# A part of one load is moved to GpSimd's queue: 1536 columns in 75, 9 and 44 partitions, after tile 53 is cast

## The chip, the cores and the metric

One core of a Trainium2 chip. The time is that of one execution on the device, in microseconds (us). The core has a TensorE (PE; its weight loads are PEld), a VectorE (DVE), a ScalarE (ACT), a GpSimd (POOL), a sync engine (SP) that issues most transfers, and 16 DMA engines that carry them. A program on fewer than eight cores has one state as a rule; all runs told of here are fast ones, and only these are compared.

## The reference

```python
def setup_inputs():
    batch, m, k, n = 16, 512, 1024, 768
    # x [16,512,1024], weight [1024,768], sub_value [16,512,768], all float32
def reference(x, weight, sub_value):
    return (np.matmul(x, weight) - sub_value).astype(np.float32)
```

Flattened, x has 8192 rows, 64 tiles of 128. The kernel reads 34 MB of x, 3 MB of weight and 25 MB of sub_value, and writes 25 MB.

## The kernel before

Eight tiles form a segment; a partition's 8 rows of a segment lie side by side in memory, so that one transfer of 8 tiles of x is 128 runs of 32 KB. The list of transfers is issued in this order by the sync engine ('x', 's', 'o' are loads of x, loads of sub_value and stores of the result; first tile, count). 'p' is the one exception: it goes to GpSimd's queue, in three parts.

```python
    ('x', 48, 8), ('s', 48, 8), ('x', 56, 7), ('p', 63, 1),
    ('o', 24, 8), ('o', 32, 8), ('s', 56, 8), ('o', 40, 8), ('o', 48, 8), ('o', 56, 5),
    ('o', 61, 2), ('o', 63, 1),
...
PARTS = (120, 125), (0, 120), (125, 128)
...
            if kind == "p":
                here, there = x_ring[:, at % NX], view(x_flat, at, 1)[:, 0]
                waits, landed["x", at] = [(counter["cast"], cast_at[at - NX]), *landed["x", at - 1]], []
                for low, high in PARTS:
                    sem = tc.alloc_semaphore(f"part{low}")
                    pool.add(lambda low=low, high=high, here=here, there=there: nc.gpsimd.dma_start(
                        out=here[low:high], in_=there[low:high], max_dma_last_dim=2048,
                    ), waits, (sem, 16))
                    landed["x", at].append((sem, 16))
                continue
```

So tile 63 of x (4 KB per partition) waits until tiles 56 to 62 have landed. ScalarE casts each tile to float16, TensorE or VectorE transposes it, TensorE multiplies, VectorE subtracts (the loads of sub_value and the stores share one ring of 32 tiles), and the sync engine stores.

## Time and profile before

| | before |
|---|---|
| median of 3 runs | 210.59 us (210.33 to 210.60) |
| span of the profiled run | 208.6 us |
| TensorE busy | 94% of the span |
| DMA | 87.08 MB at 417 GB/s |
| last matmul ends, last subtraction ends | 201.49, 202.47 us |
| last store: first and last of its 16 counts | 205.13, 207.32 us |

A transfer raises its semaphore sixteen times, once for each DMA engine that has done its share. When such counts lie far apart, some engine is behind. GpSimd's issue stands in the timeline of its engine (start, duration, what, the idle time before it and what ended it):

```profile
162.45 2.00 POOL L265 DMA_DIRECT2D x_ring<-in_x_dram  x3 [136.72 <-DMA x_ring<-in_x_dram]
```

and its landing in the list of issues (KB each, us from issue to landing):

```profile
x_ring<-in_x_dram SPq DMA_DIRECT2D x1, 3584.0 KB, 21.9
...
x_ring<-in_x_dram POOLq DMA_DIRECT2D x1, 480.0 KB, 14.7
...
x_ring<-in_x_dram POOLq DMA_DIRECT2D x1, 20.0 KB, 6.8
x_ring<-in_x_dram POOLq DMA_DIRECT2D x1, 12.0 KB, 15.8
```

One part of 120 partitions carries nearly all of it; the two small ones seem to be there to move the place at which the next part begins.

### The profile page before, as it was taken

Reading aid. Unit: us, or ns where it says so; the run is one execution under the profiler, and the core shown is the slowest. Engines: PE = TensorE matmul, PEld = TensorE weight load, DVE = VectorE, ACT = ScalarE, POOL = GpSimd, SP = SyncE. Lnnn points to the kernel's source line nnn. Section 1 sums busy time; section 2 is a strip of 40 time slices with the busy share of each in tenths; the row PEclk is TensorE's granted clock in tenths of the full one; section 3 lists DMA queues with packets and bytes.
Section 4 is the critical chain, followed back from the end, with each engine's and each line's share of the span. In section 5 each row is a group of like instructions: output and inputs, shape, how many; then the busy total and the mean of one; then the engine's idle time right before and its main releaser. Section 6 shows DMA issues by size and latency. Waiting matters only on the chain.

```text
span 208.6 us, 2617 instructions
## 1 busy us (share of the span) xinstructions
PE 195.2 (94%) x1234; PEld 75.4 (36%) x700; DVE 128.1 (61%) x224; ACT 109.0 (52%) x113; POOL 3.0 (1%) x10
## 2 busy tenths in 40 slices
PE   6899699969999999999999999999999999999960
PEld 0233244324434433443443443344344344344310
DVE  2233224975993895597399389469739938942330
ACT  2655659506573761854745676183574746516300
POOL 1000000000000000000000000000000300000000
PEclk9999999999999999999999999999999999999997
DMA  6999999999999999999999999999999999999993
GB/s 204 421 428 429 437 423 431 449 435 427 424 440 446 371 443 433 444 421 411 455 440 427 415 429 448 430 452 404 424 441 428 433 432 423 443 424 433 421 418 155
DMA packets 5685, 87.08 MB, mean 417 GB/s; under 512 B 689, under 2 KB 689, under 8 KB 2097
## 3 DMA queue, kind: packets, MB, share of 16 engines
q1 hardware_dynamic: 5472, 86.51, 97.3%
q0 software_dynamic: 208, 0.52, 0.6%
q14 instruction: 4, 0.02, 0.0%
q8 instruction: 1, 0.02, 0.0%
HBM read 61.87 MB, written 25.17 MB: 417 GB/s over the span
## 4 chain that ended last, share of the span: by engine, by line
PE 75%; DMA 13%; DVE 6%; SPq 3%; issue 1%; DVEq 0%
PE po_b L200 67%; DMA so_ring<-in_sub_value_dram 13%; PE pt_b L348 8%; DVE xtp_b L381 3%; DVE so_ring L430 2%; SPq L311 2%; SPq L275 1%; SPq L566 0%; DVEq L61 0%; SPq L140 0%
## 5 line engine op out<-in xcount | busy, mean ns | idle before, releaser
L200 PE MATMUL po_b<-w_sb,xt_b 128*128 128x384 f16 x704 | 126.0, 326 | 0.9 <-DVE w_sb L278 0.8
L430 DVE TENSOR_TENSOR so_ring<-po_b,so_ring 128x768 f32<-128x768 f32 x64 | 60.7, 957 | 58.9 <-PE po_b L200 39.8
L361 ACT COPY xt_b<-pt_b 128x1024 f16<-128x1024 f16 x44 | 44.5, 1012 | 64.7 <-PE pt_b L348 63.8
L381 DVE STREAM_TRANSPOSE xtp_b<-x16p_b 32x256 f32<-32x256 f32 x144 | 62.7, 435 | 2.3
L200 PE MATMUL po_b<-w_sb,xtp_b 128*128 128x384 f16 x320 | 61.3, 326 | 1.8 <-DVE xtp_b L381 1.7
L410 PEld LDWEIGHTS <-xt_b 128*128 128x128 f16 x352 | 34.4, 98 | 58.4 <-issue 55.2
L330 ACT CAST x_b<-x_ring 128x1024 f16<-128x1024 f32 x46 | 47.2, 1048 | 5.5 <-DMA x_ring<-in_x_dram 5.5
L348 PE MATMUL pt_b<-ident,x_b 128*128 128x128 f32 x184 | 47.6, 274 | 1.9 <-ACT x_b L330 1.9
L348 PEld LDWEIGHTS pt_b<-ident,x_b 128*128 128x128 f32 x184 | 25.3, 141 | 45.0 <-issue 36.3
L330 ACT CAST x16p_b<-x_ring 128x1024 f16<-128x1024 f32 x18 | 18.8, 1046 | 14.8 <-DMA x_ring<-in_x_dram 14.8
L410 PEld LDWEIGHTS <-xtp_b 128*128 128x128 f16 x160 | 15.7, 98 | 20.3 <-issue 18.3
L278 DVE CAST w_sb<-so_ring 128x768 f16<-128x768 f32 x8 | 4.1, 557 | 12.0 <-DMA so_ring<-in_weight_dram 12.0
L200 PE MATMUL po_b<-idle_x,idle_w 128*128 128x512 f16 x26 | 7.7, 443 | 1.7 <-POOL idle_x L180 1.7
L265 POOL DMA_DIRECT2D x_ring<-in_x_dram x3 | 2.0, 668 | 136.7 <-DMA x_ring<-in_x_dram 136.7
L361 ACT COPY xtp_b<-pt_b 128x1024 f16<-128x1024 f16 x2 | 2.0, 1012 | 2.4 <-PE pt_b L348 2.4
L330 ACT ACT_TABLE_LOAD x1 | 1.3, 1283 | 0.9 <-SPq L140 0.9
L440 PEld LDWEIGHTS <-idle_w 128*128 128x128 f16 x4 | 0.4, 100 | 1.7 <-POOL idle_x L180 1.7
L189 DVE TENSOR_TENSOR ident<-along,across 32x32 f32<-32x32 f32 x4 | 0.7, 183 | 0.1
L181 DVE MEMSET ones<- 128x32 f32 x1 | 0.1, 85 | 1.0 <-SPq L140 1.0
L180 POOL MEMSET idle_x<- 128x512 f16 x1 | 0.5, 531 | 0.0
L489 POOL MEMSET mark<- 128x1 f32 x1 | 0.1, 99 | 24.0 <-ACT xtp_b L361 24.0
L512 ACT CAST stub<-ident 128x1 f16<-128x1 f32 x2 | 0.4, 194 | 0.0
(8 smaller groups left out, 1.2 us busy)
## 6 DMA issues: line engine op xcount, KB each, us to landing
so_ring<-in_sub_value_dram SPq DMA_DIRECT2D x7, 3072.0 KB, 24.2
out_dram<-so_ring SPq DMA_DIRECT2D x7, 3072.0 KB, 26.6
x_ring<-in_x_dram SPq DMA_DIRECT2D x4, 4096.0 KB, 21.6
x_ring<-in_x_dram SPq DMA_DIRECT2D x2, 2048.0 KB, 27.2
x_ring<-in_x_dram SPq DMA_DIRECT2D x1, 3584.0 KB, 21.9
so_ring<-in_weight_dram SPq DMA_DIRECT2D x4, 768.0 KB, 8.8
x_ring<-in_x_dram SPq DMA_DIRECT2D x1, 3072.0 KB, 28.3
x_ring<-in_x_dram SPq DMA_DIRECT2D x2, 1024.0 KB, 24.8
```

Source lines behind the costliest of these rows:

```text
L189: dve.add(lambda here=here: nc.vector.tensor_tensor(out=ident[here, here], in0=along[here], in1=across[here], op=mybir.AluOpType.is_equal, ...
L200: return nc.tensor.add_instruction(mybir.InstMatmult(name=nc.get_next_instruction_name(), engine=full.engine, ins=list(full.ins), outs=lis ...
L265: pool.add(lambda low=low, high=high, here=here, there=there: nc.gpsimd.dma_start(out=here[low:high], in_=there[low:high], max_dma_last_di ...
L275: sp.add(lambda st=st, at=at: nc.sync.dma_start(out=st, in_=w_c[at]), then=(sem, 16))
L278: lambda at=at, r=r, st=st: nc.vector.tensor_copy(out=w_sb[:, at, r], in_=st[:, r]),
L311: sp.add(lambda here=here, there=there: nc.sync.dma_start(out=here, in_=there), waits, (sem, 16))
L330: act.add(lambda: nc.scalar.copy(out=to, in_=x_in), waits, count("cast"))
L348: pe.add(lambda: nc.tensor.transpose(words, from_, ident), waits, count("turn") if last else None)
L361: act.add(lambda: nc.scalar.copy(out=to, in_=pt_b[:, b]), waits, count("evac"))
L381: dve.add(lambda: nc.vector.transpose(xt[b * Q : (b + 1) * Q, :, a * Q : (a + 1) * Q], x16[a * Q : (a + 1) * Q, :, b * Q : (b + 1) * Q],), ...
L410: pe.add(lambda weights=weights: nc.tensor.ldweights(weights, tile_position=(0, 0)), [w for w in waits if w[0] in ready])
L430: dve.add(lambda: nc.vector.tensor_tensor(out=o, in0=po[:, :, :NS], in1=o, op=mybir.AluOpType.subtract), [*landed["s", mi], (counter["mul" ...
```

## The change

GpSimd takes 1536 columns instead of 1024 (1.5 tiles: half of tile 62 and tile 63), waits for a cast instead of for the landing of the load before, and deals the rows out in other parts. The intent can be read from the numbers: the parts give some DMA engines more rows than others.

```diff
-    ... ('x', 56, 7), ('p', 63, 1),
+    ... ('x', 56, 8),
-PARTS = (120, 125), (0, 120), (125, 128)
+PARTS_AT, PARTS_AFTER, PARTS_OF = 56, 53, 1536
+PARTS = (0, 75), (75, 84), (84, 128)
 ...
-            if kind == "p":            # (cut: the whole branch goes)
 ...
+            if (kind, at) == ("x", PARTS_AT):
+                here, there = here.rearrange("p j c -> p (j c)"), there.rearrange("p j c -> p (j c)")
+                whole = n * K - PARTS_OF
+                parts = [(tc.alloc_semaphore(f"part{low}"), 16) for low, _ in PARTS]
+                for t in range(at + whole // K, at + n):
+                    landed["x", t] = [*landed["x", t], *parts]
+
+                def own(here=here[:, whole:], there=there[:, whole:]):
+                    for (low, high), part in zip(PARTS, parts):
+                        pool.add(lambda low=low, high=high: nc.gpsimd.dma_start(
+                            out=here[low:high], in_=there[low:high], max_dma_last_dim=2 * PARTS_OF,
+                        ), [(counter["cast"], cast_at[PARTS_AFTER])], part)
+
+                later[PARTS_AFTER] = own
+                here, there = here[:, :whole], there[:, :whole]
 ...
+        later.pop(mi, lambda: None)()      # in cast(mi)
```

## The prediction

> **What bounds the kernel now.** I read the page from the top: busy shares, the 40 slices, the DMA queues, the chain that ended last; then the waits of the last 70 us, the windows of the tail, the landing times, and last the single DMA packets.
>
> The slices and the queue table say which resource is full:
>
> ```profile
> PE   6899699969999999999999999999999999999960
> DMA  6999999999999999999999999999999999999993
> GB/s 204 421 428 429 437 423 431 449 435 427 424 440 446 371 443 433 444 421 411 455 440 427 415 429 448 430 452 404 424 441 428 433 432 423 443 424 433 421 418 155
> q1 hardware_dynamic: 5472, 86.51, 97.3%
> q0 software_dynamic: 208, 0.52, 0.6%
> ```
>
> Two resources are full. TensorE works without a gap from about 45 us to 201.5 us, and the 16 DMA engines are at 9 tenths or more in every slice but the first and last, at some 430 GB/s. GpSimd's queue (q0) carries 0.52 MB of 87 MB.
>
> The windows and waits of the tail say which one sets the end:
>
> ```profile
> 190.00:200.00 10.00, 10.00 (x66) 3.89 (x37) 3.83 (x4) 3.98 (x4) 0.00 (x0) 1.00 1.00 428
> 200.00:208.60 8.60, 1.48 (x10) 0.29 (x3) 0.96 (x1) 0.00 (x0) 0.00 (x0) 0.84 0.61 257
> ...
> POOL x_ring L265 <- DMA x_ring<-in_x_dram: 136.7, 1, 136.7
> DVE so_ring L430 <- DMA so_ring<-in_sub_value_dram: 2.7, 1, 2.7
> SPq L537 <- DMA out_dram<-so_ring: 3.4, 1, 3.4
> ```
>
> The columns of the first two are PE, PEld, DVE, ACT, POOL, clock, DMA share, GB/s. After 200 us TensorE has 1.48 us left, while the DMA engines are still busy. The chain of work ends with the last subtraction, 201.51 to 202.47 us; yet the last store, issued at 202.50, lands 4.8 us later:
>
> ```profile
> 196.28 5.21 PE po_b L200 x32
> 201.51 0.96 DVE so_ring L430
> ...
> out_dram<-so_ring SPq DMA_DIRECT2D x1, 1920.0 KB, 10.4
> out_dram<-so_ring SPq DMA_DIRECT2D x1, 768.0 KB, 6.5
> out_dram<-so_ring SPq DMA_DIRECT2D x1, 384.0 KB, 4.8
> ```
>
> 384 KB at 430 GB/s is 0.9 us, so most of the 4.8 us is backlog. I joined the trace's DMA packets from 155 us on into 16 chains (a packet of one DMA engine starts within 4 ns of the end of the one before; only 4 of 1449 joints are irregular). No chain has a gap of note before the end: every engine works through the last three stores back to back, ending at 204.79, 204.84, 204.90, 205.00, 205.02, 205.08, 205.17, 205.21, 205.24, 205.45, 205.55, 205.73, 206.20, 206.70, 206.76 and 207.00 us. The last semaphore count is at 207.32 and the closing instructions take 1.3 us more. So **the end is set by the latest of 16 equally fast DMA engines**. Their mean end is 205.54: perfect balance would be worth 1.46 us, 0.7% of the time, and this is the only thing that the change can win, since it moves the same bytes.
>
> **What the Trainium skill says.** All four places are in "DMA: Bandwidth & Descriptors".
> - "Why a DMA increments its semaphore by 16 and not by 1": a DMA from GpSimd's queue uses the largest k up to 16 that divides its slowest dimension, on k consecutive engines from a cursor that goes round. The trace agrees: of the present parts with 5, 120 and 3 partitions, the chains show 5, 15 and 3 engines with data, and the one that has none of the 120 has a row of both small parts, as when they sit on engines 0-4, all but 4, and 4-6 (numbers counted from where the cursor began, which no record shows).
> - "Queues, rings and completion order": an engine takes turns between queues, packet by packet. The trace agrees: from 168 us on each chain alternates one 24,576-byte packet of q1 (912 ns) and one 4,096-byte packet of q0 (159 ns).
> - "Latency and other measured facts": engines 7 and 15 are usually slower. No record names an engine, but the two latest chains got neither small part, so they are among 7 to 15 (near-equal chains may be swapped at a joint, so a name can be wrong by one chain).
> - The same section: the software path's first byte comes after about 1 us. The trace differs: issue at 162.45, first q0 packet at 167.07, 4.6 us later. I use 4.6.
>
> **The change part by part.**
>
> *Removed:* the 512 KB load of tile 63 by GpSimd, which waited for tiles 56-62 to land (136.7 us of idle GpSimd that costs nothing). *Added:* 768 KB (1.5 tiles) by GpSimd in 75, 9 and 44 partitions, with the sync queue's load 1536 columns shorter.
>
> *When.* The cast of tile 53 is the 53rd of ScalarE's list, 154.42 to 155.47 us. So GpSimd issues at about 155.5 instead of 162.45, and its packets begin near 155.5 + 4.6 = 160.1, just as the sync load of 56-62 ends (160.44 median, 162.2 last). They then alternate with the stores of tiles 24-39. At 10 rows at most for an engine, a row per q1 packet, that takes 10 x (0.91 + 0.23) = 11.4 us, to about 172; if each 6 KB row is two packets of 3 KB that alternate singly, 20 x 1.03 = 20.6 us, to about 181. The casts of tiles 62 and 63, which now wait for it, start at 188.17 and 191.20. Slack of 7 us or more: **no new wait**. The first cast that needs the sync part runs at 164.48, against a landing near 162: none there either.
>
> *Cost per engine.* 24,576 bytes took 912 ns and 28,672 took 1062, so 2048 bytes less in each of 8 rows takes 8 x 0.075 = 0.60 us off every engine. A 4 KB row cost 0.155 us (159 ns less the overlap), a 6 KB row 0.230 (q1 packets of 6,144 bytes took 234; two of 3,072 at 121 come to the same). By the rule for k, 75 partitions are 15 engines with 5 rows (0-14), 9 are one each on 15 and 0-7, and 44 are 11 engines with 4 each (8-15, 0-2):
> - 0-2: 9 rows to 10: 2.30 - 1.40 - 0.60 = +0.30 us
> - 3, 5, 6: 9 to 6: 1.38 - 1.40 - 0.60 = -0.62
> - 4: 2 (and 8 empty packets) to 6: 1.38 - 0.36 - 0.60 = +0.42
> - 7: 8 to 6: 1.38 - 1.24 - 0.60 = -0.46
> - 8-14: 8 to 9: 2.07 - 1.24 - 0.60 = +0.23
> - 15: 8 to 5: 1.15 - 1.24 - 0.60 = -0.69
>
> The sum is nil within rounding, as it must be: work is dealt differently, not saved. The light engines (3-7 and 15) are plainly meant to be the late ones, and this fits the chains: 4 ends at 206.70, one of 5 and 6 at 206.20, one of 0-3 at 205.73, and the two latest are among 7-15.
>
> *Sum.* If the two latest are 7 and 15, they come to 206.1-206.5; the one of 5 and 6 to 205.6; the others stay under 206. But engine 4 loses most of the relief that it has now (2 rows instead of 8 or 9) and comes to 206.70 + 0.42 = 207.1. It would be the new last: +0.1 us. That is the catch of the change: three of the four late engines are helped, the fourth is hurt.
>
> **The rivals.**
> 1. *Engine 4 is not as late next time.* Part of its lag is in slower packets: its 24,576-byte packets took some 940 ns instead of 912 from 164 to 175 us, those of the chain ending at 206.70 likewise from 189 on, and two single ones were late by 0.32 and 0.48; together over 1 us after 160. If half of it is chance, the end is at about 206.5: -0.5 us, the balance that the author aimed at. For it: so odd a choice of 75, 9 and 44 looks like one that was measured. Against: runs before agree within 0.27 us, so the worst lag looks steady.
> 2. *The cursor begins elsewhere, or the late pair is among 8-14.* Then a late engine gets +0.23 to +0.30: the end at 207.3 or so, +0.3 us.
> 3. *A wait takes over.* The subtraction of tile 56 waits 2.7 us for its sub_value load (starts at 185.47, done 186.43); TensorE needs that bank for tile 59 at about 187.2, a slack of some 0.8 us. That load follows the GpSimd rows, so a late engine passes its lag on. By the list above it lands at 184.4-184.9 instead of 185.1, a little better. If it slipped by over 1 us, TensorE would stall, though the store backlog of 1 to 3 us behind TensorE's end would hide part: at most +0.5 us.
> 4. *The transfer is hidden anyway:* moving GpSimd's issue 7 us earlier on a full queue changes order, not the amount. That is the default: exactly 0.
>
> **Range and chances.** Default and sum give 0 to +0.1, rival 1 -0.5 (weight about a third, more than I'd give without the look of tuning), rivals 2 and 3 +0.3. From 210.59 the weighted middle is about 210.4. The hard floor is perfect balance, 209.1. An 8-in-10 range is 209.7 to 211.0. Two per cent is 4.2 us: a gain of it is three times what perfect balance gives, and a loss of it needs a stall that no slack above allows. So 1% faster, 98% same, 1% slower.
>
> **What would show it.** In the changed profile: GpSimd's issue near 155.5 with its wait on ScalarE's cast; q0 at 0.79 MB, its packets from about 160 and over by 172 (or 181); no wait of ScalarE for x after 165; TensorE's last matmul still near 201.5 and the last subtraction at 202.5, which decides that only the tail can differ; and the spread of the last store's 16 counts, now 2.2 us from first to last, smaller if the balance works, with the last at 207.3 less the gain. I am wrong if TensorE ends over 0.5 us earlier or later, if GpSimd's parts land after 188, or if the spread shrinks to under 1 us (then engine 4 was not what I take it for).

## The result, and the profile after

| | before | changed |
|---|---|---|
| median (of 4 runs each) | 210.59 us (210.33 to 210.75) | 211.60 us (211.15 to 211.94) |
| ratio | | 1.0048, 95% interval 1.0026 to 1.0070 |
| last matmul ends, last subtraction ends | 201.49, 202.47 | 201.69, 202.67 |
| last store: first and last of its 16 counts | 205.13, 207.32 | 205.05, 208.00 |

The changed kernel is slower by 1.0 us, and outside the predicted range of 209.7 to 211.0. A ratio here is the mean time of one kernel's fast runs over that of the other's of the same rounds, so not quite the ratio of the medians.

The page of the changed kernel, slices and queues as before:

```profile
PE   6999799969999999999999999999999999999950
DMA  6999999999999999999999999999999999999992
GB/s 208 417 428 430 437 427 440 459 424 421 413 485 413 377 423 451 448 413 445 445 407 424 446 437 423 456 407 429 451 411 424 436 451 413 418 423 441 417 410 112
q1 hardware_dynamic: 5472, 86.25, 96.8%
q0 software_dynamic: 208, 0.79, 0.9%
```

Nothing but the 0.79 MB in q0 is new here. GpSimd's timeline, the waits, and the landings of the last stores in the changed kernel:

```profile
155.98 2.00 POOL L311 DMA_DIRECT2D x_ring<-in_x_dram  x3 [130.52 <-ACT x16p_b L336]
```

```profile
DVE so_ring L437 <- DMA so_ring<-in_sub_value_dram: 3.1, 1, 3.1
...
SPq L544 <- DMA out_dram<-so_ring: 3.9, 1, 3.9
```

```profile
out_dram<-so_ring SPq DMA_DIRECT2D x1, 1920.0 KB, 10.9
out_dram<-so_ring SPq DMA_DIRECT2D x1, 768.0 KB, 7.0
x_ring<-in_x_dram POOLq DMA_DIRECT2D x1, 450.0 KB, 11.4
out_dram<-so_ring SPq DMA_DIRECT2D x1, 384.0 KB, 5.3
x_ring<-in_x_dram POOLq DMA_DIRECT2D x1, 264.0 KB, 16.5
```

GpSimd issues 6.5 us earlier, and its wait is now ScalarE's cast. The parts land within 16.5 us, long before the cast at 188 us that needs them. But the last three stores take 10.9, 7.0 and 5.3 us to land where they took 10.4, 6.5 and 4.8: each 0.5 us more. The subtraction of tile 56 waits 3.1 us for its sub_value instead of 2.7. No new wait appears; the same tail is longer.

**Who is last.** For this I joined the packets of the trace once more into 16 chains (one for each DMA engine: the packets that it carried, in order of time), now from 25 us on and with a rule added: in each chain the packets must come in the program's order (8 data packets and a count for each transfer of the sync queue, and the right number of rows of each of GpSimd's parts). All 16 chains then complete, with joints that are off by 0.5 ns on the mean. It corrects the chains of the prediction. In both kernels the same two engines are last:

- The very last one also carried the 16 KB instruction load in queue 8 at 30 us (933 ns, and the packet after it slow by 494 ns), which put it 1.2 to 1.5 us behind the median by 33 us in the two profiles of each kernel. At 70 us, where the load of x for tiles 24 to 31 gives way to stores, one read packet of it is slow by another 1.03 to 1.17 us in the same four profiles, more than on most of the others, and leaves it 1.8 to 2.2 us behind the median. It holds most of that lag to the end: hardly anything after 45 us lets a DMA engine rest. In the kernel before it has no row in either small part; in the changed one it has rows in the first and third part and none in the second, so it is one of engines 8 to 14 (numbered from where GpSimd's dealing begins). I call it **the last engine**.
- The second carried 8 KB instruction loads at 50 and 145 us, each costing it 0.84 us. It has a row in the first part of before (engines 0 to 3) and few rows in the changed kernel (3 to 7): engine 3.

So the last engine got 9 rows of 6 KB, not the fewer rows that I took it to have.

The last engine's way from the landing of the sub_value load of tiles 48 to 55 to that of tiles 56 to 63 holds four transfers and GpSimd's rows. It took 31.71 us before and 32.24 us changed. From there its last store ends 21.90 us later in every profile. In the kernel before it takes up the last sub_value load so (queue, bytes, start us, duration ns):

```
before : q1 4 177.66 9 | q1 24576 177.67  912 | q1 24576 178.58 912 | ... | q1 24576 184.03 1061 | q1 4 185.08 9
changed: q1 4 178.04 9 | q1 24576 178.04 1366 | q1 24576 179.40 912 | ... | q1 24576 184.85  912 | q1 4 185.76 9
```

A packet of 24,576 bytes takes 912 ns; single ones take far longer, and a slow one on the last engine is time lost for good.

### The profile page after: what moved, and what is told of

Read it like the earlier page. It is cut to its first block, busy times and chain, and to the rows that moved or that the text cites.

```text
span 209.3 us, 2616 instructions
## 1 busy us (share of the span) xinstructions
PE 195.7 (94%) x1234; PEld 75.5 (36%) x700; DVE 128.1 (61%) x224; ACT 108.8 (52%) x113; POOL 3.0 (1%) x10
## 4 chain that ended last, share of the span: by engine, by line
PE 75%; DMA 13%; DVE 6%; SPq 3%; issue 1%; DVEq 0%
PE po_b L201 67%; DMA so_ring<-in_sub_value_dram 13%; PE pt_b L355 8%; DVE xtp_b L388 3%; DVE so_ring L437 2%; SPq L317 2%; SPq L266 1%; SPq L573 0%; DVEq L62 0%; SPq L141 0%
```

## The experiments

At first three theories. **A**: only the rows dealt to the last engine count. **B**: the early issue costs. **C**: chance of a run or a chip. After the first four runs came **D**: the dealing or the size makes reads slow late. Each run stood beside the kernel before on the same chip. What I read in each, besides the ratio, is the last engine's stretch of four transfers ("stretch"), set against plain arithmetic: 7.27 us for each of three transfers, 9.68, 8.48 or 7.87 us for the load of x with 8, 7 or 6.5 tiles, and 0.155 or 0.230 us per row. What is left over is slow packets and gaps.

| run | rows on the last engine | ratio (95%) | stretch, us | left over, us |
|---|---|---|---|---|
| before (first profile) | 8 of 4 KB | 1 | 31.71 | 0.18 |
| r_before | 8 of 4 KB | 1.0008 (0.9991 to 1.0026) | 31.70 | 0.17 |
| changed (first profile) | 9 of 6 KB | 1.0048 (1.0026 to 1.0070) | 32.24 | 0.49 |
| r_after | 9 of 6 KB | 1.0054 (1.0037 to 1.0070) | 32.62 | 0.87 |
| e_ident | 8 of 6 KB | 1.0027 (1.0001 to 1.0053) | 32.54 | 1.02 |
| e_late | 9 of 6 KB | 1.0063 (1.0037 to 1.0089) | 32.90 | 1.15 |
| e_even | 8 of 6 KB | 1.0024 (1.0004 to 1.0043) | 32.70 | 1.18 |
| e_relief | 5 of 6 KB | 1.0058 (1.0038 to 1.0077) | 33.70 | 2.87 |
| e_heavy | 12 of 6 KB | 1.0061 (1.0032 to 1.0090) | 33.22 | 0.78 |
| e_early4k | 8 of 4 KB | 1.0009 (0.9990 to 1.0029) | 32.01 | 0.48 |
| f_none | none | 0.9999 (0.9986 to 1.0012) | 31.91 | 0.42 |
| f_1536 | 8 of 6 KB | 1.0025 (1.0010 to 1.0039) | 32.28 | 0.76 |
| f_1024 | 9 of 4 KB | 1.0025 (1.0011 to 1.0040) | 32.31 | 0.62 |
| f_relief4k | 5 of 4 KB | 1.0031 (1.0017 to 1.0045) | 32.01 | 0.94 |
| g_relief | 5 of 4 KB | 1.0024 (1.0011 to 1.0038) | 32.30 | 1.23 |
| g_54 | 9 of 6 KB | 1.0040 (1.0025 to 1.0054) | 32.40 | 0.65 |
| g_49 | 9 of 6 KB | 1.0131 (1.0115 to 1.0147) | 33.79 | 2.04 |

A ratio is of several runs, a stretch of one profiled run. All results were correct.

### r_before: the kernel before again (no edit)

> The kernel before, again: the floor of the comparison. All theories: a ratio of 1.000, inside 0.998 to 1.002. Its profile tells how much the lag of the latest DMA engine (last count of the last store less the mean of its 16 counts, 1.43 us in the first profile) moves from run to run: under 0.3 us if the lag is made by the program, more if it is chance.

Ratio 1.0008: the floor holds. The lag of the latest engine against the mean of the 16 was 1.68 us at the last store, 1.43 in the first profile, so it moves by 0.25 us from run to run.

### r_after: the changed kernel again (no edit)

> The changed kernel again. Theory A (dealing: the latest two engines, both among 8 to 14, have 9 rows of 6 KB where 8 rows of 4 KB and 16 KB more of the sync load were, +0.23 us) expects +0.2 to +0.4 us against before, unless the lag before the change acts is larger too. Theory B (the earlier issue collides with the sync load of tiles 56 to 62) expects the +1.0 us seen at first. Theory C (chance of a run or a chip) expects anything from 0 to +1 and a latest engine whose place among the 16 changes.

Ratio 1.0054, so the loss of 1.0 us comes back in a second set of runs, and its kin lose time on two other chips (e_even and f_1536 below): C falls. In this and all other profiles the latest is the engine with the 16 KB instruction load. Its lag was 2.32 us, 2.05 in the first profile of the changed kernel. At the end of the load of x for tiles 48 to 55 (144 us), before the change can act, the lag was 1.48 and 1.98 us in the two profiles of before and 1.78 and 1.78 in the two of the changed kernel: nearly equal on the mean. It is the last 60 us that differ.

### e_ident: eight parts that deal 8 rows to each engine

```diff
-PARTS = (0, 75), (75, 84), (84, 128)
+PARTS = (0, 9), (9, 10), (10, 11), (11, 12), (12, 13), (13, 14), (14, 16), (16, 128)
```

> The same rows in 8 parts of 9, 1, 1, 1, 1, 1, 2 and 112 partitions, which deals exactly 8 rows to each of the 16 engines and lets the profile name engines 9 to 13 one by one. Theory A: the two latest engines have 8 rows instead of 9, so 0.2 us less than the changed kernel; they show a code of one engine of 8 to 14. Theory B: no difference from the changed kernel, since GpSimd still issues at 156 us. Theory C: no difference beyond scatter, and the codes of the latest two differ from what the changed kernel's profile says.

0.7 us over before, 0.3 under the changed kernel. As a way to name engines it half failed: a part of one partition was spread over all 16 engines in packets of 384 bytes, so five of the parts mark nobody. The rest is enough. The last engine has no row in the first part (engines 0 to 8) and has one in the part of two partitions, which follows at 9: **it is engine 9 or 10**. The gain of one row, 0.23 us, is not told apart, since GpSimd's rows now last to 181 us and lie beside the last sub_value load (the mean end of the 16 engines rises from 205.60 to 206.47 us): the run changes two things.

### e_late: the issue after tile 58

```diff
-PARTS_AT, PARTS_AFTER, PARTS_OF = 56, 53, 1536
+PARTS_AT, PARTS_AFTER, PARTS_OF = 56, 58, 1536
```

> The changed kernel with GpSimd's issue only after the cast of tile 58, near 165.5 us, when the sync queue's load has landed. Parts and rows as changed. Theory A: same as the changed kernel within 0.1 us. Theory B: the loss is gone, the time of before (about 1.0 us less than the changed kernel if the first result holds). Theory C: no difference beyond scatter.

1.3 us over before: B missed. A's word, the time of the changed kernel, is not refuted by the ratio (the intervals overlap), but the profile shows another make-up. The mean end of the engines is 206.97 us, 1.4 later than in the changed kernel, while the last engine's lag shrinks to 1.55. Each of the 16 chains has slow packets in the last sub_value load, by 70 to 735 ns. A new effect, taken up with g_54 and g_49.

### e_even: one part, 8 rows on each engine

```diff
-PARTS = (0, 75), (75, 84), (84, 128)
+PARTS = (0, 128),
```

> The changed kernel with all 128 partitions in one part: 8 rows of 6 KB on each of the 16 engines. Theory A, as the profiles now shape it: the latest engine by far is the one that also carried the 16 KB instruction load at 30 us; it is engine 9 or 10, and the changed kernel deals it 9 rows. With 8 it gains one row, 0.23 us: about +0.8 us against before where the changed kernel has +1.1. Theory D (uneven dealing itself makes packets slow late, in the last sub_value load, on the engines with few rows): the slow packets at 174 to 183 us go, and the time is near before, +0.0 to +0.3 us.

0.5 us over before, 0.6 under the changed kernel. More comes back than the one row of A. But the last engine's work is now by arithmetic that of before (31.52 against 31.53 us), and 0.5 us of loss remains: in the profile it stands idle for 0.69 us before the last sub_value load, and the first packet of that load is slow by 0.47 us. A alone is not enough.

### e_relief: few rows on 9, 10 and 3

```diff
-PARTS = (0, 75), (75, 84), (84, 128)
+PARTS = (0, 4), (4, 64), (64, 72), (72, 128)
```

> Parts of 4, 60, 8 and 56 partitions: 5 rows on engines 9 and 10, 6 on engine 3 (which carries two more instruction loads), 8 or 9 on all others. Theory A: the latest engine has 4 rows less than in the changed kernel, -0.92 us for it; the end is then set by engine 3 or by the rest, about 0.6 to 0.9 us under the changed kernel, +0.2 to +0.4 against before. Theory D: engines 3, 9 and 10 get slow packets in place of their relief, and the end moves by less than 0.3 us.

This is the plainest refutation of A. The dealing worked: the last engine shows 5 rows and came to the last sub_value load with a lag of 1.24 us instead of 1.87. Then that load took 9.84 us on it instead of 7.3: 238 ns of idle time, a first packet slow by 1070 ns, two more by 363 and 861. The load lands so late that the subtraction of tile 56 waits far longer, TensorE's last matmul ends at 203.07, and other engines stand idle before the last store. The wait in the profile of e_relief, where the changed kernel has 3.1:

```profile
DVE so_ring L437 <- DMA so_ring<-in_sub_value_dram: 4.6, 1, 4.6
```

Four rows less should give 0.92 us; the time is that of the changed kernel. Relief was given back.

### e_heavy: 12 rows on 9 and 10

```diff
-PARTS = (0, 75), (75, 84), (84, 128)
+PARTS = (0, 18), (18, 67), (67, 122), (122, 128)
```

> Parts of 18, 49, 55 and 6 partitions: 12 rows on engines 9 and 10, 7 or 8 on the others. Theory A: 3 rows more on the latest engine than in the changed kernel, 0.7 us slower than it, about +1.7 us against before. Theory D: nearly even for the 14 others, so no slow packets on them, and no slower than the changed kernel.

1.3 us over before: slower than the changed kernel as A wants, but by about 0.2 and not 0.7 us. The interval (1.0032 to 1.0090) is too wide to exclude either none or 0.7. In the profile the rows do what arithmetic says (stretch 33.22 against 32.24 and 32.62); D's word that it would be no slower fits the ratio, but the reason it gave does not: slow packets came on nine engines here too.

### e_early4k: the early issue with the load of before

```diff
-PARTS_AT, PARTS_AFTER, PARTS_OF = 56, 53, 1536
-PARTS = (0, 75), (75, 84), (84, 128)
+PARTS_AT, PARTS_AFTER, PARTS_OF = 56, 53, 1024
+PARTS = (0, 5), (5, 125), (125, 128)
```

> The issue of the changed kernel (after the cast of tile 53) with the load of before: 1024 columns (tile 63 alone) in 5, 120 and 3 partitions, so the same rows on the same engines as before, 7 us earlier. Theory A: engine 9 or 10 has the work of before, so the time of before, or up to 0.2 us less as GpSimd's rows no longer lie beside the last sub_value load. Theory B (the earlier issue costs): the loss of the changed kernel, +0.6 to +1.0 us.

1.0009, with before inside the interval. **The earlier issue is not what costs**: B falls.

### f_none: no load by GpSimd

```diff
-    ... ('x', 56, 7), ('p', 63, 1),
+    ... ('x', 56, 8),
```

(in the kernel before)

> The kernel before without any load by GpSimd: the sync queue loads all 8 tiles of 56 to 63. Even work on all 16 engines and no second queue. If the dealing of before is worth something (it spares engine 4 alone, which is not the last one), this is slower than before by 0.2 to 0.5 us; if the last engine alone decides, it is as before within 0.2 us.

0.9999. The whole device of a second queue and three parts is worth nothing measurable in the kernel before: the engine that it spares (engine 4, with 2 rows) is not the one that ends last.

### f_1536 and f_1024: size and dealing apart

f_1536:

```diff
-PARTS = (0, 75), (75, 84), (84, 128)
+PARTS = (0, 5), (5, 125), (125, 128)
```

> 1536 columns as in the changed kernel, issued after tile 53 as in it, but dealt as before, in 5, 120 and 3 partitions. The last engine, 9 or 10, has 8 rows, the work of before to the nanosecond. Theory A (only its rows count): the time of before, +0.0 to +0.2 us. Theory D (more bytes through GpSimd's queue bring slow packets in the last sub_value load): as the even dealing, +0.4 to +0.6 us.

f_1024:

```diff
-PARTS_AT, PARTS_AFTER, PARTS_OF = 56, 53, 1536
+PARTS_AT, PARTS_AFTER, PARTS_OF = 56, 53, 1024
```

> 1024 columns as before, issued after tile 53, but dealt as in the changed kernel, in 75, 9 and 44 partitions. Theory A: one row of 4 KB more on the last engine, +0.15 us, so +0.3 to +0.4 against before with the +0.2 that the early issue alone showed. Theory D: the size makes the loss, so +0.2 like the early issue alone. With the other three this fills a square of size and dealing: if the two effects simply add, the changed kernel's +1.1 is the size's share plus the dealing's.

With e_early4k and the changed kernel this fills a square, all with the issue after tile 53:

| | dealt 5, 120, 3 | dealt 75, 9, 44 |
|---|---|---|
| 1024 columns | 1.0009 | 1.0025 |
| 1536 columns | 1.0025 | 1.0048 and 1.0054 |

Size adds 0.16% and dealing 0.16%, 0.34 us each; together with the 0.09% of the corner that is 1.0041, a little under the 1.005 measured. Both theories hit one run and missed the other: f_1536 has the last engine's work of before, and A said no loss; f_1024 has the size of before, and D said no loss. The intervals are wide for this: a difference of two corners is good to some 0.5 us (estimated from the widths of the intervals). So 0.16% is not told apart from none. From either corner of 1.0025 to the changed kernel it is 0.23 and 0.29%, and only the two measurements of the changed kernel taken together put that outside the error. That size and dealing both count is likely; how much each does is not shown.

### f_relief4k: few rows on the last engine, with 1024 columns

```diff
-PARTS_AT, PARTS_AFTER, PARTS_OF = 56, 53, 1536
-PARTS = (0, 75), (75, 84), (84, 128)
+PARTS_AT, PARTS_AFTER, PARTS_OF = 56, 53, 1024
+PARTS = (0, 4), (4, 64), (64, 72), (72, 128)
```

> 1024 columns, issued after tile 53, in 4, 60, 8 and 56 partitions: 5 rows on engines 9 and 10, 6 on 3, 8 or 9 on the rest. Theory A: 3 rows of 4 KB off the last engine, 0.46 us under the early issue alone, so 0.2 to 0.3 us under before. If relief is given back in the last sub_value load, as 1536 columns showed, it is +0.2 us or more.

0.6 us over before where rows alone promise a gain. In the profile 0.83 us were lost in one packet at 159.7 us, when the last engine was still reading x and the others began to store.

### g_relief: the same dealing in the kernel before

```diff
-PARTS = (120, 125), (0, 120), (125, 128)
+PARTS = (0, 4), (4, 64), (64, 72), (72, 128)
```

> The kernel before with its own wait (GpSimd issues at 162.4 us, after tiles 56 to 62 have landed) and its own 1024 columns, dealt in 4, 60, 8 and 56 partitions: 5 rows in place of 8 on the last engine. If rows alone count here: 3 x 0.155 = 0.46 us less than before, a ratio of 0.998. If the last engine gives relief back in slow reads of the last sub_value load, as with the early issue: 1.000 or above.

1.0024: given back again, without any early issue. Here all 16 engines have slow packets in the last sub_value load, up to 322 ns, while GpSimd's rows lie beside it; and one packet of the last engine is slow by 405 ns at 159.5 us, before GpSimd has issued anything. So a part of the slow reads is no work of GpSimd's rows.

### g_54 and g_49: the changed kernel, issued after tiles 54 and 49

```diff
-PARTS_AT, PARTS_AFTER, PARTS_OF = 56, 53, 1536
+PARTS_AT, PARTS_AFTER, PARTS_OF = 56, 54, 1536
```

> The changed kernel (1536 columns, 75, 9 and 44 partitions) with GpSimd's issue after tile 54, near 163.6 us, where before issues (162.4), so that its rows lie from 168 to 179 us. If issuing early is what makes the last engine's reads slow, they go back to the 0.15 us of before and the loss falls from +1.0 to the one row's +0.2 to +0.3. If the rows beside the last sub_value load slow all engines instead, as in the run with tile 58, the mean of the 16 ends rises by 0.5 us or more and the time is +1.0 to +1.3.

```diff
-PARTS_AT, PARTS_AFTER, PARTS_OF = 56, 53, 1536
+PARTS_AT, PARTS_AFTER, PARTS_OF = 56, 49, 1536
```

> The changed kernel with GpSimd's issue after tile 49, near 148.6 us, so that its rows lie from 153 to 165 us, beside the load of tiles 56 to 62 itself. If rows beside a load slow all engines, the mean at the landing of that load rises over the changed kernel's by 0.5 us and the time with it: +1.3 or more. If it is only the last sub_value load and its lag that count, about the changed kernel's +1.0.

Issued at 164.0 us, near where before issues, the changed kernel still loses 0.8 us; issued at 149 it loses 2.7. The second half of the expectation of g_54 (the mean end of the 16 rose by 0.87 us; the time rose by a little less than the 1.0 to 1.3 named) and the first of g_49 came true, and the windows show it. The stretches are those of the load of x (152 to 160 us), of the stores (162 to 174) and of the last sub_value load (174 to 184); the last two columns are DMA share and GB/s. First the changed kernel (rows at 160 to 173 us), then e_late (rows from 170.7 us on), g_54 (rows at 169 to 182 us), and g_49 (rows at 153 to 167 us):

```profile
152.00:160.00 8.00, 8.00 (x55) 3.52 (x33) 5.23 (x9) 5.87 (x6) 2.00 (x3) 1.00 0.98 422
162.00:174.00 12.00, 12.00 (x79) 4.59 (x43) 7.44 (x12) 7.48 (x8) 0.00 (x0) 1.00 1.00 429
174.00:184.00 10.00, 10.00 (x65) 3.73 (x35) 8.74 (x18) 5.12 (x7) 0.00 (x0) 1.00 1.01 420
```

```profile
162.00:174.00 12.00, 12.00 (x79) 4.59 (x43) 7.45 (x12) 7.48 (x9) 2.00 (x3) 1.00 1.01 435
174.00:184.00 10.00, 10.00 (x66) 3.80 (x36) 8.65 (x18) 5.03 (x7) 0.00 (x0) 1.00 1.02 367
```

```profile
174.00:184.00 10.00, 10.00 (x65) 3.81 (x36) 8.60 (x18) 4.97 (x7) 0.00 (x0) 1.00 1.02 392
```

```profile
152.00:160.00 8.00, 8.00 (x54) 3.59 (x32) 5.32 (x9) 5.87 (x6) 0.00 (x0) 1.00 1.07 359
162.00:174.00 12.00, 12.00 (x79) 4.59 (x43) 7.44 (x12) 7.58 (x9) 0.00 (x0) 1.00 1.01 428
```

The DMA engines are as busy in every line, yet they move 367, 392 and 359 GB/s where GpSimd's rows lie beside a load, against 420 or more otherwise. In the chains of g_49 the packets of the x load are slow by 230 to 600 ns as long as rows are in turn with them, on every engine. Beside the stores of the changed kernel a row costs its own 234 ns, and the 912 ns of the store's packets stay. **In these runs a second queue that reads memory beside a load slows both; beside a store it does not.** The changed kernel puts nearly all of its rows beside stores. Of the four places tried only tile 49 is told apart in time, as the worst; the intervals of tiles 53, 54 and 58 (1.0, 0.8 and 1.3 us over before) overlap. The loss of the changed kernel is not this effect: the mean end of its 16 engines is 205.60 us, against 205.54 in before.

## Why the prediction was wrong

- *The end is set by the latest of 16 equally fast DMA engines; the same bytes only change their spread.* Right. TensorE's end moved by 0.2 us (all of it is there at 144 us, before the change acts), and the spread of the last store's counts went from 2.2 to 2.95 us.
- *No new wait; GpSimd issues at 155.5, packets from 160.1.* Right: 155.98, and packets from 160.19 to 173.46 us, one 6,144-byte packet per row.
- *The cost of a row and the deal of rows to engines.* Right: the chains show 5, 1 and 4 rows where the rule for k puts them.
- *"If the two latest are 7 and 15, they come to 206.1-206.5".* **This step failed.** The last engine is 9 or 10 and the next is 3. The line of the prediction for engines 8 to 14, +0.23 us, was the one to apply to the last engine, and rival 2 named this case and gave it "the end at 207.3 or so". I leaned on the look of the parts (light engines must be the late ones) and on the word of the Trainium skill on engines 7 and 15 that the prediction names, while the chains only said "7 to 15" and, for want of the order rule, had even that wrong for one of the two.
- *A term was missing.* In the profiles the last engine's stretch grew by 0.53 and 0.92 us over before's 31.71, 0.73 on the mean, and its last store ends 0.75 us later on the mean (207.67 and 208.09 against 207.00 and 207.27). One row more is 0.23 of it. The other 0.5 are slow reads: 454 and 830 ns in the two profiles, against 149 and 134 before. No such term stood in my sum. The medians differ by 1.0 us, 0.3 more than the profiled runs; only profiled runs leave a trace, so that remainder is not placed.
- *"Engine 4 ... would be the new last".* Wrong: it ended at 205.67 and 205.82 us (one engine in each profile shows packets of 945 ns instead of 912 in stores; in before it is engine 4, and by these I know it again). Its lag came in at -0.14 and -0.04 us against the mean of the 16, where the first profile of before had +0.62: the lag that I took as its own was half a run's chance. Engine 3, which the change did relieve (by 0.62 us in the list), lost 1.4 to 1.6 us to slow reads and gained nothing.
- *Rival 3, the sub_value load lands later.* Right in kind: the subtraction of tile 56 started at 186.15 instead of 185.47. It stayed hidden in the changed kernel behind the stores' backlog.

**What stays open** is why single reads of the late engines are slow. They come at the turn from a load to stores, when the late engine still reads and the others already write, and at its first read after stores, in nearly every kernel tried, f_none included, but amount to 0.15 us in both profiles of before and to 0.4 to 0.9 in most others. The size and the dealing shift the engines against each other, and relief of a late engine is regularly lost again. That the amount hangs on how the engines stand to each other is my guess; no run here shows the mechanism.

No version beat both kernels. The plainest one, f_none, equals the kernel before without GpSimd's part.

## What to carry to other kernels

When all DMA engines are full to the end, find out which of them is last and why (here an instruction load at 30 us and a slow read at 70 us that no later stage absorbs) before dealing work around it; a name inferred from the shape of someone's tuning is no finding. Check that a relief survives the next transfers, because a time saved in one stage can be lost in slow packets of the next. Put the reads of a second queue beside stores, not beside loads.

## What the Trainium skill lacked or had wrong

- "DMA: Bandwidth & Descriptors", "Issuing engines are not separate DMA queues": it says that queues share the 16 engines and interleave. The runs add that it matters what they interleave with: rows of a second queue beside a load brought the core to between 359 and 392 GB/s with busy engines, against 429 and 435 beside stores.
- The same page, "Latency and other measured facts": engines 7 and 15 usually slower. This case gives no sign of it, but can't refute it, since no record names an engine: counted from the start of GpSimd's dealing, the last two in both kernels are 9 or 10, and 3, which lie 6 or 7 apart and so can't be 7 and 15, and their lag begins with instruction loads. The engine so counted as 15 ended at 205.98 and 205.82 us in the changed kernel, 1.7 us or more ahead of the last.
- The same section: about 1 us to the first byte for the software path. On a full queue it took 4.6 us before and 4.2 us in the changed kernel.
- No page tells what an instruction load costs the DMA engine that carries it (it would belong to "Runtime: NRT & Kernel Launch", "Instruction fetch mechanics"): 16 KB at 30 us took 933 ns and slowed the packet after it by 494 ns, 8 KB took 309 ns and slowed one by 530, and the lag stayed for the rest of the kernel.
